# Four buffers for the split weight halves, and no page of its own for the modulation sums

## The chip, the cores and the metric

The kernel runs on one core of a Trainium2 chip. The metric is the device time in microseconds of one execution. Five engines work from queues of their own, each in the order in which the compiler put its instructions: TensorE (PE, matmuls), VectorE (DVE), ScalarE (ACT), GpSimd (POOL) and SyncE (SP), which here issues nearly all DMA transfers.

## The reference

One block of a diffusion transformer: 512 latent tokens and 256 context tokens of width 2048, all in float32.

```python
mod = silu(c) @ w_mod + b_mod                 # six chunks of 2048: shift, scale, gate (mixer), shift, scale, gate (MLP)
h = rms_norm(x, nw0) * (1 + sc_m) + sh_m      # the same for the context
p = concat(h_ctx, h_lat) @ w_in               # 2048 -> 6176
lru = conv + gated linear recurrence, both directions
gdn = conv + chunked gated delta rule, 8 heads, both directions
x = x + g_m * rms_norm(concat(lru, gdn) @ w_out, nw1)
h = rms_norm(x, nw2) * (1 + sc_f) + sh_f
x = x + g_f * rms_norm(square(relu(h @ w_ff1)) @ w_ff2, nw3)      # 2048 -> 8192 -> 2048
```

The two shift and scale rows of the mixer (chunks 0 and 1) are needed first. The other four chunks are needed later: chunk 2 scales the mixer's output, chunks 3 and 4 the MLP's input, and chunk 5 (`g_f`) only the very last sum.

## The kernel before

**Products.** Every float32 product is made of three matmuls in a rounded format (`fp32r`): each operand is split into a high and a low part, and high x high, high x low and low x high are added in one PSUM bank. For the weights the split is done on the fly. A weight piece `wr` of 128 x 1024 is loaded by SP, and each of its two halves is turned into `wh` (a cast on ACT, line 67) and `wl` (a subtraction on DVE or POOL, line 61). In the mixer's input product and in the MLP one half feeds 12 matmuls, in the output product 6. The text calls the matmuls of one half a quarter.

**The feed.** Class `Feed` (line 475) makes the halves in order for the input product, the output product and the first two MLP blocks. Before the first product it splits three halves; after the products of half c, `next` splits half c + 3 into the buffers that half c has just left, since `wh` and `wl` have three buffers each. The other MLP blocks do the same through `wpiece` (line 276), and the first modulation chunks in a loop of their own (line 328).

**Pages.** Most temporary tiles are "pages" of 128 x 512 float32, 29 buffers of one tag. A few kinds have tags of their own: five buffers `ld` for loads, four for the recurrent state, and one, `macc`, for the modulation sums.

**Modulation sums.** `modacc` (line 1144) makes one quarter f of chunks 2 to 5. It takes a tile, clears it on POOL (line 1148), loads a row of `b_mod` into it (line 1149) and adds 16 rows of weights to it with 16 DVE operations (line 64), each fed by one `ld` load of 256 KB (line 1156). For chunks 2, 3 and 4 (12 sums, made during the mixer) the running sum lies in a PSUM bank: only the first of the 16 operations reads the tile, and a copy on ACT (line 1164) brings the sum back into it at the end. For chunk 5 the sum stays in the tile. Then the tile is stored to DRAM (`accD`, line 1165). The next sum clears the same buffer, so it waits for that store.

**The gate rows.** `modrow(5, 3)` (line 1173) is called in the MLP's loop at block b == 3, right behind the call that makes the four sums of chunk 5. It loads each sum back and multiplies it with a matrix of ones (line 1181, four matmuls on PE), to spread it over all partitions. The result is used only by the last 16 sums of the kernel.

**What sets the order.** A planner in the kernel spawns the tasks of the mixer between the quarters (`slot`), and marks at each `boundary` keep an engine from running more than one to three slots ahead. The MLP from its third block on, and the sums of chunk 5, have no such marks: there the framework's scheduler places each instruction when its inputs and a buffer are there in its own model of time, and otherwise by the order of the program. Once placed, the order on an engine is fixed.

Of the kernel before, what the change touches and what calls it, by code (L numbers as in the profile page):

```python
# [8 lines left out]
F32R = mybir.dt.float32r  # L9
# [7 lines left out]
P = 128  # L17
# [14 lines left out]
def build(tc, A, out, stop=None, dump=None):  # L32
    nc = tc.nc
    V, S, G, T, SP = nc.vector, nc.scalar, nc.gpsimd, nc.tensor, nc.sync
    es = ExitStack()
    with es:
        cp = es.enter_context(tc.tile_pool(name="const", bufs=1))
        wp = es.enter_context(tc.tile_pool(name="weights", bufs=2))
        pp = es.enter_context(tc.tile_pool(name="pages", bufs=29))
        ld_n = 5  # L40

        pg = ps = es.enter_context(tc.tile_pool(name="psum", bufs=8, space=PSUM))
# [3 lines left out]
        def nm(s):  # L46
            cnt[0] += 1
            return f"{s}_{cnt[0]}"

        def page(dt=F32, tag="pg", shape=(P, 512), bufs=None):  # L50
            kw = {} if bufs is None else {"bufs": bufs}
            return pp.tile(list(shape), dt, tag=tag, name=nm(tag), **kw)

        def bank(pool=None, tag="b"):
            return (pool or ps).tile([P, 512], F32, tag=tag, name=nm("bk"))
# [7 lines left out]
        def stt(out, a, s, b, op0, op1):  # L63
            V.scalar_tensor_tensor(out=out, in0=a, scalar=s, in1=b, op0=op0, op1=op1)

        def split(src, hi, lo, lo_eng=None):
            S.copy(hi, src)  # L67
            tt(lo_eng or V, lo, src, hi.bitcast(F32), ALU.subtract)
# [43 lines left out]
        def mload(j):  # L112
            if j < len(mpieces):
                f, kind, k = mpieces[j]
                col = kind * D + f * 512
                mraw[j] = quad("mr", F32)
                SP.dma_start(mraw[j], wmod[:, k:k + 4, col:col + 512])
# [32 lines left out]
        def columns(src, n, dst):  # L150
            b = bank()
            T.transpose(b[:, :n], src[:n, :], ident[:n, :n])
            V.tensor_copy(dst[:, :n], b[:, :n])
# [122 lines left out]
        def wpiece(src, nk, cols, eng=(V, V)):  # L276
            r = wp.tile([P, 1024], F32, tag="wr", name=nm("wr"), bufs=3)
            rv = r[:, :nk * cols].rearrange("p (k f) -> p k f", f=cols)
            SP.dma_start(rv, src)
            res = []  # L280
            n = nk * cols // 2
            for i in range(2):
                h = wp.tile([P, 512], F32R, tag="wh", name=nm("wh"), bufs=3)
                l = wp.tile([P, 512], F32R, tag="wl", name=nm("wl"), bufs=3)
                split(r[:, i * n:(i + 1) * n], h[:, :n], l[:, :n], eng[i])
                hv, lv = (x[:, :n].rearrange("p (k f) -> p k f", f=cols) for x in (h, l))
                res += [(hv[:, k, :], lv[:, k, :]) for k in range(nk // 2)]
            return res
# [15 lines left out]
        def mod_cols(f, kind, pm):  # L304
            mrow, nrow = page()[:4], page()[:2]
            V.tensor_copy(mrow, pm[0][:4, :])
            S.copy(nrow, pm[1][:2, :])
            yield
            b = bank()
            bv = b[:, 0:8].rearrange("p (k j) -> p k j", j=2)  # L310
            for k in range(4):
                T.matmul(bv[:, k, :], mrow[:, k * P:(k + 1) * P], sel, start=True, stop=False)
                T.matmul(bv[:, k, :], nrow[:, k * P:(k + 1) * P], ident[:2, :2], start=False, stop=True)
            dst = (shc, scol)[kind][:, :, 4 * f:4 * f + 4]
            bm = bmod[:, kind * 16 + 4 * f:kind * 16 + 4 * f + 4]
            for j in range(2):
                tt(V, dst[:, j, :], bv[:, :, j], bm, ALU.add)
                if kind == 1:
                    stt(dst[:, j, :], dst[:, j, :], 1.0, nw0[:, 4 * f:4 * f + 4], ALU.add, ALU.mult)
            if kind == 1:  # L320
                for t in range(2):
                    yield
                    ts_ = slice(t * P, (t + 1) * P)
                    to_fm(xctx[t][f], [x[:, :, ts_] for x in Hc[f][0]], [x[:, :, ts_] for x in Hc[f][1]],
                          scol[:, 1, 4 * f:4 * f + 4], shc[:, 1, 4 * f:4 * f + 4])

        late = []
        for j, (f, kind, k0) in enumerate(mpieces):
            if k0 == 0:
                pm = [bank(pg), bank(pg)]  # L330
            r = mraw.pop(j)
            hl = []
            for i in range(3):
                h = wp.tile([P, 512], F32R, tag="wh", name=nm("wh"), bufs=3)
                l = wp.tile([P, 512], F32R, tag="wl", name=nm("wl"), bufs=3)
                split(r[:, i], h, l)
                hl.append((h, l))
            T.matmul(pm[1][:2, :], csn[:, k0 + 3, :], r[:, 3], start=k0 == 0, stop=k0 == 12)
            for i in range(3):
                k = k0 + i  # L340
                T.matmul(pm[0][:4, :], cst[:, k, :], hl[i][0], start=k == 0, stop=False)
                T.matmul(pm[0][:4, :], cst[:, k, :], hl[i][1], start=False, stop=k == 14)
            del hl, h, l
            mload(j + MB)
            if j == 2:
                while vs:
                    columns(*vs.pop(0))
            for g in list(late):
                if next(g, 0) == 0:
                    late.remove(g)  # L350
            if k0 == 12:
                late.append(mod_cols(f, kind, pm))
                next(late[-1])
        while late:
            for g in list(late):
                if next(g, 0) == 0:
                    late.remove(g)
# [35 lines left out]
        class Task:  # L393


            def __init__(self, gen, order=0, rate=None, prio=0):
                self.gen, self.order, self.rate, self.credit, self.wait, self.done = gen, order, rate, 0.0, 0, False
                self.urgent, self.prio = False, prio
# [76 lines left out]
        class Feed:  # L475
            def __init__(self, pieces):
                self.pieces, self.raws, self.parts, self.c = pieces, {}, {}, 0
                for j in range(3):
                    self.load(j)
                for c in range(3):  # L480
                    self.split(c)

            def load(self, j):
# [6 lines left out]
            def split(self, c):  # L490
                if c >= 2 * len(self.pieces):
                    return
                _, nk, cols, eng = self.pieces[c // 2]
                n = nk * cols // 2
                r = self.raws[c // 2][:, (c % 2) * n:(c % 2) * n + n]
                h = wp.tile([P, 512], F32R, tag="wh", name=nm("wh"), bufs=3)[:, :n]
                l = wp.tile([P, 512], F32R, tag="wl", name=nm("wl"), bufs=3)[:, :n]
                split(r, h, l, eng[c % 2])
                self.parts[c] = (h, l)
                if c % 2:  # L500
                    del self.raws[c // 2]
                    self.load(c // 2 + 3)
# [2 lines left out]
                return self.parts.pop(self.c)  # L505

            def next(self):
                self.split(self.c + 3)
                self.c += 1

        def run_tiles(ds):
# [632 lines left out]
        def modacc(chunk, f, after=None):  # L1144

            col = chunk * D + f * 512
            acc = seed = page(tag="macc", bufs=1)
            G.memset(acc, 0.0)
            SP.dma_start(acc[0:1, :], A["b_mod"][:, col:col + 512])
            if after is None:  # L1150
                acc = bank()
            q = []
            for k in range(17):
                if k < 16:
                    w = page(tag="ld", bufs=ld_n)
                    SP.dma_start(w, wmod[:, k, col:col + 512])
                    q.append(w)
                if k > 0:
                    stt(acc, q.pop(0), silc[:, k - 1:k], seed if k == 1 else acc, ALU.mult, ALU.add)
                    if after is not None:  # L1160
                        tc.add_manual_dep(nc.cur_bb.bb.instructions[-1], after, NOSYNC, reason="order")
                    yield 0.7, 0, 0
            if after is None:
                S.copy(seed, acc)
            SP.dma_start(accD[4 * (chunk - 2) + f], seed)
            modok.add((chunk, f))
# [90 lines left out]
        for o in orders[0] + orders[1]:  # L1257
            for k in o[1]:
                c = o[0]
# [15 lines left out]
        def big4(i):  # L1275
            if i < 3:
                xs = [pp.tile([P, 1024], F32, tag="A", name=nm("big"), bufs=A_BUFS) for _ in range(2)]
                return [xs[c // 2][:, c % 2 * 512:c % 2 * 512 + 512] for c in range(4)]
            return [page(tag="S", bufs=4) for _ in range(4)]
# [260 lines left out]
        acc = [big4(t) for t in range(4)]  # L1540
# [53 lines left out]
```

## Time and profile before

| what | value |
|---|---|
| median of 3 runs | 2808.57 us (2805.38 to 2812.1) |
| the profiled execution's own time | 2803.51 us |
| its span, first to last instruction | 2801.7 us |
| PE busy | 2654.4 us, 95% of the span |
| DVE, ACT, POOL busy | 1682.8, 1187.9, 586.1 us |
| mean granted clock of PE | 0.979 |

The page names an instruction by line, engine and operation, then output and inputs by tile name. A time in square brackets behind a row is how long the engine had been idle before it, and what ended that. The stages follow each other as: modulation chunks 0 and 1 (to about 140 us), input product and mixer (to about 1240), output product (to about 1380), MLP (to the end).

### The profile page before, as it was taken

Reading aid. Unit: us, or ns where it says so; the run is one execution under the profiler, and the core shown is the slowest. Engines: PE = TensorE matmul, PEld = TensorE weight load, DVE = VectorE, ACT = ScalarE, POOL = GpSimd, SP = SyncE. Lnnn points to the kernel's source line nnn. Section 1 sums busy time; section 2 is a strip of 40 time slices with the busy share of each in tenths; the row PEclk is TensorE's granted clock in tenths of the full one; section 3 lists DMA queues with packets and bytes.
Section 4 is the critical chain, followed back from the end, with each engine's and each line's share of the span. In section 5 each row is a group of like instructions: output and inputs, shape, how many; then the busy total and the mean of one; then the engine's idle time right before and its main releaser. Section 6 shows DMA issues by size and latency. Waiting matters only on the chain.

```text
span 2801.7 us, 39553 instructions
## 1 busy us (share of the span) xinstructions
PE 2654.4 (95%) x14253; PEld 2178.3 (78%) x14253; DVE 1682.8 (60%) x3287; ACT 1187.9 (42%) x2418; POOL 586.1 (21%) x552
## 2 busy tenths in 40 slices
PE   6989899899999998988999999999999999999998
PEld 2378797788777887776898887888888888888886
DVE  5786767777696777847598433444433444334436
ACT  4556576654556564535552222222222222222223
POOL 1155354344244354326310000000000000000002
PEclk9999999999999999989999999999999999999999
DMA  9664465566566667646778333333333333333335
GB/s 331 215 177 126 109 187 166 153 187 190 168 189 189 200 198 222 212 150 212 235 258 277 119 98 113 98 98 98 98 98 98 94 96 97 98 98 98 98 98 154
DMA packets 374968, 434.33 MB, mean 155 GB/s; under 512 B 22665, under 2 KB 212450, under 8 KB 374770
## 3 DMA queue, kind: packets, MB, share of 16 engines
q1 hardware_dynamic: 373984, 431.59, 49.6%
q8 instruction: 112, 1.84, 0.3%
q14 instruction: 86, 0.70, 0.1%
q10 hardware_dynamic: 786, 0.19, 0.0%
HBM read 401.31 MB, written 30.41 MB: 154 GB/s over the span
## 4 chain that ended last, share of the span: by engine, by line
PE 57%; DVE 4%; DMA 2%; POOL 1%; issue 1%; ACT 1%; SPq 0%; DVEq 0%; ACTq 0%; POOLq 0%
PE bk L1510 8%; PE bk L1508 8%; PE bk L1509 8%; PE bk L1497 7%; PE bk L1498 7%; PE bk L1499 7%; PE bk L1420 2%; PE bk L1419 2%; PE bk L1418 2%; PE bk L1469 1%; DVE pg L61 1%; PE bk L1468 1%; PE bk L1467 1%; DVE wl L61 1%; PE bk L524 1%
## 5 line engine op out<-in xcount | busy, mean ns | idle before, releaser
L67 ACT CAST wh<-wr 128x512 fp32r<-128x512 f32 x952 | 584.6, 618 | 1217.1 <-PE bk L1498 443.9
L61 DVE TENSOR_TENSOR wl<-wr,wh 128x512 fp32r<-128x512 f32 x642 | 464.1, 725 | 761.6 <-ACT wh L67 643.3
L61 POOL TENSOR_TENSOR wl<-wr,wh 128x512 fp32r<-128x512 f32 (+1 forms) x310 | 402.4, 1304 | 609.9 <-ACT wh L67 555.1
L1510 PE MATMUL bk<-wl,pg 128*128 128x512 f32 x960 | 373.6, 389 | 0.9 <-DVE wl L61 0.9
L1509 PE MATMUL bk<-wh,pg 128*128 128x512 f32 x960 | 373.5, 389 | 0.0
L1508 PE MATMUL bk<-wh,pg 128*128 128x512 f32 x960 | 373.5, 389 | 0.0
L1497 PE MATMUL bk<-H2h,wh 128*128 128x512 f32 x896 | 349.9, 390 | 0.0
L1499 PE MATMUL bk<-H2h,wl 128*128 128x512 f32 x896 | 349.0, 390 | 0.0
L1498 PE MATMUL bk<-H2l,wh 128*128 128x512 f32 x896 | 349.0, 390 | 0.0
L524 PE MATMUL bk<-Hlh,wh 128*128 128x512 f32 (+1 forms) x784 | 316.5, 404 | 0.0
L526 PE MATMUL bk<-Hlh,wl 128*128 128x512 f32 (+1 forms) x784 | 309.9, 395 | 1.8 <-POOL wl L61 1.8
L525 PE MATMUL bk<-Hll,wh 128*128 128x512 f32 (+1 forms) x784 | 310.1, 396 | 0.0
L61 POOL TENSOR_TENSOR big<-big,pg 128x512 f32<-128x512 f32 x9 | 12.0, 1340 | 1247.5 <-ACT pg L1570 1247.5
L1510 PEld LDWEIGHTS bk<-wl,pg 128*128 128x128 f32 x960 | 180.2, 188 | 38.8 <-DVE wl L61 1.3
L1508 PEld LDWEIGHTS bk<-wh,pg 128*128 128x128 f32 x960 | 180.2, 188 | 37.3
L1509 PEld LDWEIGHTS bk<-wh,pg 128*128 128x128 f32 x960 | 180.2, 188 | 37.2
L1498 PEld LDWEIGHTS bk<-H2l,wh 128*128 128x128 f32 x896 | 168.5, 188 | 35.4 <-issue 0.5
L1497 PEld LDWEIGHTS bk<-H2h,wh 128*128 128x128 f32 x896 | 168.6, 188 | 35.3 <-issue 0.2
L1499 PEld LDWEIGHTS bk<-H2h,wl 128*128 128x128 f32 x896 | 168.5, 188 | 35.2
L526 PEld LDWEIGHTS bk<-Hlh,wl 128*128 128x128 f32 (+1 forms) x784 | 148.4, 189 | 35.8 <-POOL wl L61 2.3
L524 PEld LDWEIGHTS bk<-Hlh,wh 128*128 128x128 f32 (+1 forms) x784 | 149.1, 190 | 30.9 <-ACT pg L1071 0.2
L525 PEld LDWEIGHTS bk<-Hll,wh 128*128 128x128 f32 (+1 forms) x784 | 148.8, 190 | 29.9
(346 smaller groups left out, 4514.5 us busy)
## 6 DMA issues: line engine op xcount, KB each, us to landing
wr<-in_w_ff SPq DMA_DIRECT2D x272, 512.0 KB
wr<-in_w_in SPq DMA_DIRECT2D x144, 512.0 KB
ld<-in_w_mod SPq DMA_DIRECT2D x256, 256.0 KB
mr<-in_w_mod SPq DMA_DIRECT2D x32, 1024.0 KB
wr<-in_w_out SPq DMA_DIRECT2D x64, 512.0 KB
pg<-vkD SPq DMA_DIRECT2D x88, 128.0 KB
ld<-in_x SPq DMA_DIRECT2D x32, 256.0 KB
vkD<-pg SPq DMA_DIRECT2D x24, 256.0 KB
```

Source lines behind the costliest of these rows:

```text
L61: e.tensor_tensor(out=out, in0=a, in1=b, op=op)
L67: S.copy(hi, src)
L524: T.matmul(pt[:m, :n], wh, a, start=k == 0, stop=False)
L525: T.matmul(pt[:m, :n], wh, b, start=False, stop=False)
L526: T.matmul(pt[:m, :n], wl, a, start=False, stop=k == 15)
L1418: T.matmul(bk[t], mh[:, s_], h, start=st, stop=False)
L1497: T.matmul(bk[c], w[kk][0][:, s_], hh, start=k == 0, stop=False)
L1498: T.matmul(bk[c], w[kk][0][:, s_], hl_, start=False, stop=False)
L1499: T.matmul(bk[c], w[kk][1][:, s_], hh, start=False, stop=k == 15)
L1508: T.matmul(o, ah, h, start=k == 0, stop=False)
L1509: T.matmul(o, al, h, start=False, stop=False)
L1510: T.matmul(o, ah, l, start=False, stop=k == 3)
```

## The change

Three things are changed.

1. `wh` and `wl` have four buffers each in place of three. The feed splits four halves before the first product, and half c + 4 after the products of half c.
2. The tag `macc` is gone. The modulation sums take an ordinary page. For chunks 2 to 4 that page is let go after the first of the 16 operations, and the copy at the end takes another page.
3. The ordinary pages are 28 in place of 29, which makes up, with the `macc` page, for the two added buffers.

```diff
-        pp = es.enter_context(tc.tile_pool(name="pages", bufs=29))
+        pp = es.enter_context(tc.tile_pool(name="pages", bufs=28))
...
-                h = wp.tile([P, 512], F32R, tag="wh", name=nm("wh"), bufs=3)
-                l = wp.tile([P, 512], F32R, tag="wl", name=nm("wl"), bufs=3)
+                h = wp.tile([P, 512], F32R, tag="wh", name=nm("wh"), bufs=4)
+                l = wp.tile([P, 512], F32R, tag="wl", name=nm("wl"), bufs=4)
...
-                for c in range(3):
+                for c in range(4):
                     self.split(c)
...
             def next(self):
-                self.split(self.c + 3)
+                self.split(self.c + 4)
                 self.c += 1
...
         def modacc(chunk, f, after=None):
 
             col = chunk * D + f * 512
-            acc = seed = page(tag="macc", bufs=1)
+            acc = seed = page()
             G.memset(acc, 0.0)
             SP.dma_start(acc[0:1, :], A["b_mod"][:, col:col + 512])
             if after is None:
                 acc = bank()
...
                 if k > 0:
                     stt(acc, q.pop(0), silc[:, k - 1:k], seed if k == 1 else acc, ALU.mult, ALU.add)
+                    if after is None:
+                        seed = None
                     if after is not None:
                         tc.add_manual_dep(nc.cur_bb.bb.instructions[-1], after, NOSYNC, reason="order")
                     yield 0.7, 0, 0
             if after is None:
+                seed = page()
                 S.copy(seed, acc)
             SP.dma_start(accD[4 * (chunk - 2) + f], seed)
```

Instructions move with it, mostly by one split: on each engine the split of a half stands one quarter earlier among the other work. At three places more than that moves.

**The sums of chunk 5 on DVE.** Before, the 64 operations of line 64 (`macc<-ld,silc,macc`) stand scattered from the first MLP blocks on. Here are the first of them, beside the halves `wl` of the second MLP block:

```order
L61 TENSOR_TENSOR wl_15281<-wr_15146,wh_15280 128x512
L61 TENSOR_TENSOR pg_15259<-pg_15257,pg_15258 128x256
L64 SCALAR_TENSOR_TENSOR macc_17336<-ld_17339,silc,macc_17336 128x512
L61 TENSOR_TENSOR wl_15299<-wr_15190,wh_15298 128x512
L64 SCALAR_TENSOR_TENSOR macc_17336<-ld_17341,silc,macc_17336 128x512
L61 TENSOR_TENSOR wl_15315<-wr_15190,wh_15314 128x512
```

The last of the 64 then stands beside the 609th half, 55 halves ahead of the one whose products PE does just before the gate rows (the 664th; halves are counted from the kernel's first). With the change the first of the sums stands behind the 656th half, in the products of the MLP's third block with `w_ff2`:

```order
L61 TENSOR_TENSOR big_15822<-big_15822,bk_17046 128x512
L61 TENSOR_TENSOR S_15824<-S_15824,bk_17047 128x512
L61 TENSOR_TENSOR wl_17165<-wr_17158,wh_17164 128x512
L64 SCALAR_TENSOR_TENSOR pg_17348<-ld_17351,silc,pg_17348 128x512
L64 SCALAR_TENSOR_TENSOR pg_17348<-ld_17353,silc,pg_17348 128x512
L64 SCALAR_TENSOR_TENSOR pg_17348<-ld_17356,silc,pg_17348 128x512
L61 TENSOR_TENSOR wl_17203<-wr_17200,wh_17202 128x512
```

From there 27 of them stand among 12 halves and 12 sums of the MLP's output (`big`, `S`). The other 37 stand in one run behind `wl_17633`, the 668th half, whose beginning is:

```order
L64 SCALAR_TENSOR_TENSOR pg_17400<-ld_17429,silc,pg_17400 128x512
L61 TENSOR_TENSOR wl_17629<-wr_17626,wh_17628 128x512
L64 SCALAR_TENSOR_TENSOR pg_17400<-ld_17432,silc,pg_17400 128x512
L61 TENSOR_TENSOR wl_17633<-wr_17626,wh_17632 128x512
L64 SCALAR_TENSOR_TENSOR pg_17400<-ld_17435,silc,pg_17400 128x512
L64 SCALAR_TENSOR_TENSOR pg_17400<-ld_17438,silc,pg_17400 128x512
L64 SCALAR_TENSOR_TENSOR pg_17400<-ld_17441,silc,pg_17400 128x512
```

and whose end is:

```order
L64 SCALAR_TENSOR_TENSOR pg_17504<-ld_17548,silc,pg_17504 128x512
L64 SCALAR_TENSOR_TENSOR pg_17504<-ld_17551,silc,pg_17504 128x512
L61 TENSOR_TENSOR pg_17562<-bk_17560,ld_17558 128x512
L61 TENSOR_TENSOR pg_17570<-bk_17568,ld_17566 128x512
L61 TENSOR_TENSOR pg_17578<-bk_17576,ld_17574 128x512
L61 TENSOR_TENSOR pg_17586<-bk_17584,ld_17582 128x512
L61 TENSOR_TENSOR wl_17663<-wr_17660,wh_17662 128x512
```

The four rows `pg<-bk,ld` take the results of the gate rows, so the last sum now stands just ahead of the gate rows' use. SP's queue moved with it: 59 of the 64 `ld` loads stand among the weight pieces of the same stretch, and the last 32 of them between two neighbouring weight pieces.

**The gate rows on PE.** Their place did not move. With the change (line 1184 is the old 1181, lines 1500 to 1502 the old 1497 to 1499, 1512 and 1513 the old 1509 and 1510):

```order
L1512 MATMUL bk_17275<-wh_17316,pg_16431 128x512
L1513 MATMUL bk_17275<-wl_17317,pg_16430 128x512
L1184 MATMUL bk_17560<-ld_17556,ones 128x512
L1184 MATMUL bk_17568<-ld_17564,ones 128x512
L1184 MATMUL bk_17576<-ld_17572,ones 128x512
L1184 MATMUL bk_17584<-ld_17580,ones 128x512
L1500 MATMUL bk_17588<-H2h_13512,wh_17594 128x512
```

`wh_17316` is the 664th half, `wh_17594` the 665th: the gate rows stand between the third block's second product and the next block's first.

**A modulation sum of the mixer on DVE.** The first operation of the sixth of the 12 sums (chunk 3), at about 713 us in the trace, stands before the change like this (`negL` and `ss` are rows of the delta rule and of a norm):

```order
L61 TENSOR_TENSOR pg_7683<-pg_7683,bk_7716 128x512
L64 SCALAR_TENSOR_TENSOR bk_7816<-ld_7817,silc,macc_7813 128x512
L64 SCALAR_TENSOR_TENSOR pg_7763<-bk_7764,negL,pg_7668 128x128 x4
L745 TENSOR_SCALAR ss_7751<-ss_7751 128x8
L64 SCALAR_TENSOR_TENSOR bk_7816<-ld_7819,silc,bk_7816 128x512
```

and with the change like this:

```order
L61 TENSOR_TENSOR pg_7693<-pg_7693,bk_7724 128x512
L64 SCALAR_TENSOR_TENSOR pg_7773<-bk_7774,negL,pg_7678 128x128 x4
L745 TENSOR_SCALAR ss_7761<-ss_7761 128x8
L185 TENSOR_SCALAR rqy_7806<-ss_7761 128x8
L64 SCALAR_TENSOR_TENSOR rqt_7807<-rqy_7806 128x8
```

The first operation (`bk_7825<-ld_7826,silc,pg_7822`) now stands 16 other operations later, behind the whole norm. The second and the third of the 12 sums moved in the same way by 16 and 12 operations, the fifth by 11, the seventh 13 earlier; the other seven by one at most.

More of the change, by code (lines that the diff above doesn't have):

```diff
@@ L333, in build @@
             for i in range(3):
-                h = wp.tile([P, 512], F32R, tag="wh", name=nm("wh"), bufs=3)
-                l = wp.tile([P, 512], F32R, tag="wl", name=nm("wl"), bufs=3)
+                h = wp.tile([P, 512], F32R, tag="wh", name=nm("wh"), bufs=4)
+                l = wp.tile([P, 512], F32R, tag="wl", name=nm("wl"), bufs=4)
                 split(r[:, i], h, l)
@@ L495, in split @@
                 r = self.raws[c // 2][:, (c % 2) * n:(c % 2) * n + n]
-                h = wp.tile([P, 512], F32R, tag="wh", name=nm("wh"), bufs=3)[:, :n]
-                l = wp.tile([P, 512], F32R, tag="wl", name=nm("wl"), bufs=3)[:, :n]
+                h = wp.tile([P, 512], F32R, tag="wh", name=nm("wh"), bufs=4)[:, :n]
+                l = wp.tile([P, 512], F32R, tag="wl", name=nm("wl"), bufs=4)[:, :n]
                 split(r, h, l, eng[c % 2])
```

## The prediction

> **What bounds the kernel now.** I read the page first, then who PE waited for, then PE's own rows in order of time.
>
> ```profile
> span 2801.7 us, 39553 instructions
> PE 2654.4 (95%) x14253; PEld 2178.3 (78%) x14253; DVE 1682.8 (60%) x3287; ACT 1187.9 (42%) x2418; POOL 586.1 (21%) x552
> ...
> PE bk L255 <- DVE pg L64: 19.8, 7, 5.7
> PE bk L951 <- DVE pg L927: 11.8, 4, 9.2
> PE bk L526 <- POOL wl L61: 8.8, 9, 1.8
> PE bk L524 <- ACT wh L67: 4.2, 6, 1.3
> PE bk L1420 <- POOL wl L61: 3.5, 4, 1.3
> PE bk L342 <- DVE wl L61: 3.4, 7, 0.8
> PE bk L1469 <- DVE wl L61: 3.4, 5, 1.4
> PE bk L526 <- DVE wl L61: 3.2, 4, 1.2
> PE bk L1181 <- DMA ld<-accD: 2.6, 1, 2.6
> PE bk L1510 <- DVE wl L61: 0.9, 1, 0.9
> ```
>
> PE sets the end: it is idle for 147 us (2801.7 - 2654.4) and works the rest. Each row of the waits gives the total, the number and the longest. The seven rows on `wh` and `wl` are what a fourth buffer can touch, and they sum to 27.4 us, 1% of the span. The other waits are for chains of DVE (transposes, the delta rule). So the buffers alone are worth little, and anything else that the change moves by tens of us decides.
>
> The rows of PE show where it stands, and windows show its pace and clock (columns: window, PE busy and count, PEld, DVE, ACT, POOL, granted clock, DMA share, GB/s):
>
> ```profile
> 480.45 0.36 PE L578 MATMUL bk<-pg,pg 128*128 128x256 f32 x1 [2.66 <-DVE pg L61]
> ...
> 720.21 0.77 PE L578 MATMUL bk<-pg,pg 128*128 128x512 f32 x1 [2.13 <-DVE pg L64]
> ...
> 1080.99 0.31 PE L951 MATMUL bk<-pg,A 32*32 32x32 f32 x4 [9.23 <-DVE pg L927]
> ...
> 1693.99 2.74 PE L1181 MATMUL bk<-ld,ones 128*128 128x512 f32 x6
> 1699.31 1.54 PE L1181 MATMUL bk<-ld,ones 128*128 128x512 f32 x2 [2.58 <-DMA ld<-accD]
> ...
> 1701.08 0.63 PE L1498 MATMUL bk<-H2l,wh 128*128 128x512 f32 x1
> ...
> 1238.00:1246.00 8.00, 7.55 (x21) 5.58 (x20) 1.69 (x3) 1.85 (x4) 2.74 (x3) 0.51 0.01 3
> 1699.00:1704.00 5.00, 4.69 (x12) 3.23 (x13) 1.05 (x2) 0.00 (x0) 0.00 (x0) 0.66 0.79 252
> 2000.00:2400.00 400.00, 400.00 (x1766) 331.23 (x1765) 172.76 (x267) 113.40 (x187) 0.00 (x0) 1.00 0.32 98
> ```
>
> In the long MLP stretch PE never waits and does a matmul in 400 / 1766 = 0.2265 us, so a quarter of 12 takes 2.72 us. A buffer more gains nothing there. After a wait the clock is about half for a while: between 1699 and 1704 us the mean is 0.66, so of 5 us 0.34 x 5 = 1.7 us are lost; 8 us at 0.51 (1238 to 1246) lose 3.9.
>
> **Part 1: the fourth buffer.** It adds no instruction; it lets a split run one quarter earlier. That quarter is 2.72 us in the MLP's full rows, half of that where the rows have 256 columns or a half feeds 6 matmuls. Every wait in the seven rows is at most 1.8 us long, near or under this, so nearly all single ones should go. I leave out the 3.4 us of L342: that stage has DMA as its bound, by the second of these rows.
>
> ```profile
> DMA  9664465566566667646778333333333333333335
> GB/s 331 215 177 126 109 187 166 153 187 190 168 189 189 200 198 222 212 150 212 235 258 277 119 98 113 98 98 98 98 98 98 94 96 97 98 98 98 98 98 154
> ```
>
> Of the other 24.0 us I keep 3 for places in the context rows where several waits follow each other, since there the split is short of throughput and one buffer is used up once: 21. The clock falls after a wait, too: for the three longest of them (1.8, 1.4, 1.4) I add an estimated 1.7 us each, from the row at 1699: 5. Together -26, with 0 and -29 (24.0 + 5) as its ends.
>
> **Part 2: the modulation sums of the mixer.** Before, the next sum had to wait until the last was stored.
>
> ```profile
>   DMA accD<-macc: 94.7, 10
> ...
>   DMA macc<-in_b_mod: 16.0, 5
> ...
> 472.26 1.76 DVE L64 SCALAR_TENSOR_TENSOR bk<-ld,silc,macc 128x512 f32<-128x512 f32 x1 [4.61 <-DMA macc<-in_b_mod]
> ...
> 718.36 0.76 DVE L64 SCALAR_TENSOR_TENSOR bk<-ld,silc,macc 128x512 f32<-128x512 f32 x1 [4.93 <-DMA macc<-in_b_mod]
> ```
>
> The first two rows say what POOL and DVE waited for at this tile: POOL stood 94.7 us before the clearing, with `wl` halves queued behind it, and DVE 16.0 us for the row of biases. Two of PE's waits follow directly: 480.45 and 720.21, after DVE's 4.61 and 4.93 us. The page ends the wait for the store, and in the order two of these first operations stand 16 others later, so DVE should not meet them early any more. That is 2.66 + 2.13, and 1.7 of clock at each: -8. The L951 group behind the 9.23 us wait stands 13 to 16 matmuls later now, about 3.5 us: -3.5.
>
> What it costs: a page must be free twice per sum, where one had lain ready. The trace has no page wait. From above I bound it by DVE's 16.0 us at the old tile, from below by 0, and take 0, since few other rows moved in the mixer.
>
> Parts 1 and 2 are -38 at most of their likely values. Some is given back: what PE does not lose on a weight it may lose at the next DVE chain, and DVE is packed before 1081 us. I take half, -19, with ends at -38 and -4.
>
> **Part 3: the sums of chunk 5.** This term decides.
>
> ```profile
> L64 DVE SCALAR_TENSOR_TENSOR macc<-ld,silc,macc x64: 741/750/754, 1434.1 to 1541.5; 128x512 f32<-128x512 f32 x64
> ...
> 1499.66 2.32 DVE L64 SCALAR_TENSOR_TENSOR macc<-ld,silc,macc 128x512 f32<-128x512 f32 x3
> 1501.89 0.68 DVE L61 TENSOR_TENSOR wl<-wr,wh 128x512 fp32r<-128x512 f32 x1
> 1502.50 2.32 DVE L64 SCALAR_TENSOR_TENSOR macc<-ld,silc,macc 128x512 f32<-128x512 f32 x3
> ...
> 1541.50 0.75 DVE L64 SCALAR_TENSOR_TENSOR macc<-ld,silc,macc 128x512 f32<-128x512 f32 x1 [1.22 <-DMA ld<-in_w_mod]
> ...
> 1670.74 1.88 DVE L61 TENSOR_TENSOR big<-big,bk 128x512 f32<-128x512 f32 x3
> 1672.54 0.68 DVE L61 TENSOR_TENSOR S<-S,bk 128x512 f32<-128x512 f32 x1
> 1673.14 0.68 DVE L61 TENSOR_TENSOR wl<-wr,wh 128x512 fp32r<-128x512 f32 x1
> ...
> 1517.78 0.33 SPq L1165 DMA_DIRECT2D accD<-macc  x1
> 1521.04 0.53 POOL L1148 MEMSET macc<- 128x512 f32 x1 [25.06 <-DVE S L1514]
> ...
> 1537.24 0.46 SPq L1156 DMA_DIRECT2D ld<-in_w_mod  x1
> ...
> 1695.77 0.34 SPq L1170 DMA_DIRECT2D ld<-accD  x1
> ```
>
> Before, the 64 operations ended at 1542 us, 150 us ahead of the gate rows at 1694. In the new order they begin behind the 656th half. With four buffers its cast waits for the products of the 652nd, 12 quarters before the gate rows: 1694.0 - 12 x 2.72 = 1661.4. Four sums of the output (2.40 us, 1670.74 to 1673.14), the cast and the subtraction later, 1664.8, the first one starts. Per operation DVE needs (1501.89 - 1499.66) / 3 = 0.74 us, per half 0.61 (1501.89 to 1502.50), per sum of the output 0.60. So up to the run of 37: 27 x 0.74 + 12 x 0.61 + 12 x 0.60 = 34.5, to 1699.3. PE came to the gate rows at 1694.0 and stands.
>
> The run: DVE alone needs 37 x 0.74 = 27.4. But each operation needs a load into one of five buffers. From issue (1537.24) to use (1541.50) one took 4.3 us, and the load of a sum 3.5 (1695.77 to 1699.31). With the operation and the issue, 0.74 + 0.2, five loads go round in 4.4 to 5.2 us: 0.9 to 1.05 each. I take 0.95 for the 32 that are not there yet: 32 x 0.95 + 5 x 0.74 = 34, to 1733.4. Ends: 27.4, and 49 at the pace of the old stretch, 43 us for 32 operations by this window of the tile:
>
> ```profile
> 1499.50:1542.50 43.00, 23.99 (x32) 0.00 (x0) 0.53 (x1) 1.00 0.82 274
> ```
>
> The Trainium skill (DMA: Bandwidth & Descriptors, Specifications) gives about 358 GB/s of HBM bandwidth per core; by that a load of 256 KB takes 0.73 us, DVE would set the pace, the run would take 27.4 us and the forecast would be 6.6 us lower. The highest slice here shows 331 GB/s, 0.79 us a load, but round trips with five buffers bind first.
>
> After the run come store and reload: 3.3 us (1517.78 to 1521.04) and 3.5. The last gate row then runs at 1740.2 and PE goes on at 1741, where it went on at 1701.1: +40. The clock stays low somewhat longer than after the old 2.58 us wait, between 0 and 2.2 us (3.9 - 1.7): +1. The Trainium skill (TensorE: Matmul & The Clock Gate, Part 1) has full clock back after one busy window of about 3.4 us, which would make it 0; the 8 us at 0.51 differ from that. Nothing covers these 41 us, because PE's next product stands behind the gate rows. Ends: +33 and +56.
>
> **Sum.** +41 - 19 = +22. The profiled execution took 2803.5 us (2801.7 of span and 1.8 around it): 2825.5. The three timed runs have a median 5.1 us higher, so for the median 2830.
>
> **The rivals.** (a) PE never stands at the gate rows, because the 64 operations come early enough, and only the gains stay: 2808.6 - 19 = 2790, faster. It needs them done within the 32.6 us of the 12 quarters; DVE alone would need 64 x 0.74 = 47. Against it stand all rows above; for it only that waits could let DVE run ahead. 5%. (b) Gains whole, run at DVE's pace: -38 + 33 (+2 for stragglers) leaves 2806, no change. For it speaks that PE's weight waits are spread and mostly local. 9%. (c) Pages bind in the mixer: 12 sums with a page wait at each end, 24 waits of 0.7 us or more on DVE's or ACT's queue, 16 us: 2846. Against: ACT's and POOL's other rows kept their order. 12%. (d) The buffers and the page do nothing, since DVE's chains take all back: 2808.6 + 41 - 4 = 2846. 13%. My forecast: 61%.
>
> **Numbers.** 0.2% (5.6 us) is about what a measurement tells from no change here. Faster: (a), and 1% of the forecast's low tail, 6%. No change: (b), 9%. Slower: 85%. The forecast's own range is 2815 to 2846 (part 3 from +33, gains from -30; part 3 +52, gains -14); with (b), (c) and (d) 2807 to 2853 holds 8 in 10.
>
> **What would show it.** Right: at L1184 (the old L1181) one wait of about 40 us for a load of `accD`, behind an unbroken run of L64 on DVE with PE idle; waits for `wh` and `wl` down from 27.4 to some 6 us; no wait of DVE or POOL for a store of the old sum. Wrong: the gate rows without a wait over 10 us, or operations of chunk 5 before 1600 us; new waits for pages at the clearing or the copy; weight waits as before.

## The result: 1.6% slower

The changed kernel takes 2850.43 us (median of 4 runs, 2849.47 to 2851.32), the kernel before 2806.98 us in the same comparison: a ratio of 1.0161, 95% interval [1.0141, 1.0182], about +43 us. Foretold were 2830 us (+22) and a range of 2807 to 2853. The direction and the one large term were right; the gain that was to pay for half of it did not come. The measured time lies 3 us inside this range and outside the forecast's own, 2815 to 2846.

The page of the changed kernel gives its span, PE's work and PE's granted clock in 40 slices:

```profile
span 2849.6 us, 39560 instructions
PE 2665.5 (94%) x14253; PEld 2192.1 (77%) x14253; DVE 1690.8 (59%) x3287; ACT 1185.5 (42%) x2418; POOL 582.2 (20%) x552
PEclk8999899999999999989999997999999999999999
```

The span grew by 47.9 us. PE does the same 14253 matmuls in 11.1 us more of busy time (2665.5 against 2654.4) and is idle for 184.1 us in place of 147.3. The slice with a 7 in the clock is the place of the new wait.

What PE waited for in the changed kernel (total, number, longest), the rows of the gate rows, of DVE's chains and of the weight halves. The output product's lines 1418 to 1420 are 1421 to 1423 now, and 1467 to 1469 are 1470 to 1472:

```profile
PE bk L1184 <- DMA ld<-accD: 40.5, 3, 39.0
PE bk L255 <- DVE pg L64: 24.9, 7, 8.2
PE bk L1038 <- DVE pg L64: 9.3, 3, 4.8
PE bk L1423 <- DVE wl L61: 4.9, 3, 3.3
PE bk L526 <- DVE wl L61: 4.3, 3, 2.5
PE bk L342 <- DVE wl L61: 4.2, 9, 0.8
PE bk L524 <- ACT wh L67: 0.8, 1, 0.8
PE bk L1423 <- POOL wl L61: 0.7, 1, 0.7
PE bk L1472 <- DVE wl L61: 0.6, 2, 0.4
PE bk L526 <- POOL wl L61: 0.2, 1, 0.2
```

The seven rows on `wh` and `wl` sum to 15.7 us where the seven rows quoted of before summed to 27.4. So the fourth buffer did take waits for weights away. That is less than forecast, where some 6 us were to be left. The longest of those left are longer (3.3 and 2.5 us, before 1.8), and the transposes of line 255 wait 5 us more for DVE in the row shown.

**At the gate rows.** PE's rows of the changed kernel around them:

```profile
1702.43 0.39 PE L1513 MATMUL bk<-wl,pg 128*128 128x512 f32 x1
1741.86 2.08 PE L1184 MATMUL bk<-ld,ones 128*128 128x512 f32 x2 [39.03 <-DMA ld<-accD]
1745.13 3.98 PE L1184 MATMUL bk<-ld,ones 128*128 128x512 f32 x4 [1.19 <-DMA ld<-accD]
1749.33 1.22 PE L1184 MATMUL bk<-ld,ones 128*128 128x512 f32 x2 [0.23 <-DMA ld<-accD]
1749.98 0.79 PE L1500 MATMUL bk<-H2h,wh 128*128 128x512 f32 x1
1750.62 0.40 PE L1501 MATMUL bk<-H2l,wh 128*128 128x512 f32 x1
```

and what DVE did meanwhile (the 64 operations of chunk 5, then the beginning and the end of the unbroken run):

```profile
L64 DVE SCALAR_TENSOR_TENSOR pg<-ld,silc,pg x64: 744/752/754, 1671.6 to 1740.9; 128x512 f32<-128x512 f32 x64
...
1707.51 3.91 DVE L64 SCALAR_TENSOR_TENSOR pg<-ld,silc,pg 128x512 f32<-128x512 f32 x5
1712.58 2.33 DVE L64 SCALAR_TENSOR_TENSOR pg<-ld,silc,pg 128x512 f32<-128x512 f32 x3 [1.15 <-DMA ld<-in_w_mod]
...
1737.76 3.90 DVE L64 SCALAR_TENSOR_TENSOR pg<-ld,silc,pg 128x512 f32<-128x512 f32 x5 [0.37 <-DMA ld<-in_w_mod]
```

PE came to the gate rows at 1702.8 and did the second matmul behind them (line 1501, before 1498) at 1750.62, 47.8 us later; before it came at 1693.99 and did the same matmul at 1701.08, 7.1 us later. The difference is 40.7 us. The run lasted from 1707.5 to 1741.7, 34.1 us for 37 operations.

What the first gate row waited for is its reload, not its sum. SP's rows of the four stores and reloads, the first and the last of each:

```profile
1690.38 0.33 SPq L1168 DMA_DIRECT2D accD<-pg  x1
...
1738.54 0.33 SPq L1173 DMA_DIRECT2D ld<-accD  x1
...
1741.69 0.33 SPq L1168 DMA_DIRECT2D accD<-pg  x1
...
1746.44 0.32 SPq L1173 DMA_DIRECT2D ld<-accD  x1
```

The first sum was stored at 1690.38, before PE came. Its reload was issued only at 1738.54, because it stands behind the loads of chunk 5 on SP's queue. The last gate row then waited for the last sum, stored at 1741.69.

**Ahead of the gate rows.** PE reached them 8.8 us later than before (1702.8 against 1694.0) where 19 us earlier was forecast. Windows of PE show what that is made of (window, busy and count, granted clock, DMA share, GB/s), first before, then the changed kernel:

```profile
0.00:300.00 300.00, 251.46 (x1453) 0.95 0.65 207
300.00:600.00 300.00, 274.85 (x1875) 0.96 0.53 155
600.00:1400.00 800.00, 744.36 (x4573) 0.97 0.64 198
...
0.00:1693.99 1693.99, 1560.62 (x9445) 0.97 0.61 190
```

```profile
0.00:300.00 300.00, 255.01 (x1452) 0.91 0.65 207
300.00:600.00 300.00, 269.29 (x1817) 0.93 0.52 150
600.00:1400.00 800.00, 744.72 (x4528) 0.97 0.64 196
...
0.00:1702.80 1702.80, 1570.23 (x9445) 0.96 0.59 182
```

The last row of each counts the same 9445 matmuls, up to the gate rows: PE was idle for 1693.99 - 1560.62 = 133.4 us before and 1702.80 - 1570.23 = 132.6 us after. Idle time is the same within 1 us, although 12 us of waits for weights went: they came back as other waits. Up to the gate rows the sum of PE's waits by what ended them is, without those for `wh` and `wl`, 3.8 us larger for DVE, 5.6 for DMA and 3.0 for ACT and POOL together. And the same matmuls took 9.6 us more of busy time. The clock was lower in two stages: 0.91 for 0.95 up to 300 us, 0.93 for 0.96 from 300 to 600. By the counts the first of them cost next to nothing, since PE had done 1452 matmuls at 300 us and 1453 before; from 300 to 600 us it did 58 fewer, from 600 to 1400 us 45 fewer.

One row stands out in the second of these stages. DVE and POOL of the changed kernel, beside PE's next wait:

```profile
413.43 1.30 POOL L61 TENSOR_TENSOR wl<-wr,wh 128x512 fp32r<-128x512 f32 x1 [5.11 <-DMA ld<-in_w_mod]
...
417.44 0.54 POOL L1148 MEMSET pg<- 128x512 f32 x1
417.93 5.05 POOL L61 TENSOR_TENSOR wl<-wr,wh 128x512 fp32r<-128x512 f32 x4
422.93 1.28 POOL L61 TENSOR_TENSOR pg<-ld,pg 128x512 fp32r<-128x512 f32 x1
...
419.41 7.25 DVE L64 SCALAR_TENSOR_TENSOR bk<-ld,silc,pg 128x512 f32<-128x512 f32 x1 [4.83 <-DMA pg<-in_b_mod]
...
427.57 2.08 PE L1038 MATMUL bk<-pg,A 128*128 128x128 f32 x8 [4.84 <-DVE pg L64]
```

An operation that has a median of 0.76 us in this kernel and 1.9 us at most in the kernels without this event took 7.25 us, beside an unbroken stretch of POOL in which four `wl` halves stand in a row; PE then waited 4.84 us. Comparing when PE reached the same matmul, the changed kernel was 3.5 us behind before the event (416 us) and 10.7 us behind after it (444 us). The distance does not stay so: it is 14.1 us at 555 us and 4.6 us at 1088 us, and 8.8 us at the gate rows.

### The profile page after: what moved, and what is told of

The parts are those of the page before. It is cut to its first block, busy times and chain, and to the rows that moved or that the text cites. A ratio compares the mean times of both kernels' runs of the same rounds, so it can differ in the third digit from the quotient of the medians.

```text
span 2849.6 us, 39560 instructions
## 1 busy us (share of the span) xinstructions
PE 2665.5 (94%) x14253; PEld 2192.1 (77%) x14253; DVE 1690.8 (59%) x3287; ACT 1185.5 (42%) x2418; POOL 582.2 (20%) x552
## 4 chain that ended last, share of the span: by engine, by line
PE 50%; DVE 2%; DMA 1%; issue 0%; POOL 0%; ACT 0%; DVEq 0%; SPq 0%; ACTq 0%; POOLq 0%
PE bk L1511 8%; PE bk L1512 8%; PE bk L1513 8%; PE bk L1501 7%; PE bk L1500 7%; PE bk L1502 7%; DMA ld<-in_w_mod 1%; PE bk L1472 1%; PE bk L1470 1%; PE bk L1471 1%; DVE pg L64 1%; PE bk L1423 1%; PE bk L1422 1%; PE bk L1421 1%; DVE wl L61 0%
## 5 line engine op out<-in xcount | busy, mean ns | idle before, releaser
L61 POOL TENSOR_TENSOR big<-big,pg 128x512 f32<-128x512 f32 x9 | 11.5, 1296 | 1206.3 <-ACT pg L1573 1206.3
```

What stands on the lines that cost most here:

```text
L61: e.tensor_tensor(out=out, in0=a, in1=b, op=op)
```

## The experiments

Each was compared with the kernel before on the same chip. Theory G is about the gate rows, the theories M, B, P and C (the clock) about the rest.

**Chunk 5 on a tag of its own.** The changed kernel with one line more, and a page less:

```diff
-        pp = es.enter_context(tc.tile_pool(name="pages", bufs=28))
+        pp = es.enter_context(tc.tile_pool(name="pages", bufs=27))
...
-            acc = seed = page()
+            acc = seed = page() if after is None else page(tag="macc", bufs=1)
```

> The changed kernel, but the four sums of chunk 5 get a tag of their own with one buffer again (the mixer's sums stay on ordinary pages; 27 ordinary pages make up for it). In the order the 64 operations stand beside halves 558 to 609 again, as before the change. Theory G (the 39 us wait at the gate rows comes from these operations standing behind half 655): the wait falls from 39 us to under 5 us and the time from 2850 to about 2811. Theory M (the rest of the loss, 8.8 us up to the gate rows, comes with the fourth buffer or with the mixer's pages): 2811 to 2816 remain, above the 2807 of before. Prediction as it stood (mixer gains 19): 2790. Rival to G (the gate rows wait for something else, the reload itself): the wait stays over 30 us and the time near 2850.

Measured: 2808.88 us, ratio 1.0017 [1.0003, 1.0030]. Its gate rows:

```profile
1698.40 2.74 PE L1184 MATMUL bk<-ld,ones 128*128 128x512 f32 x6
1704.25 1.24 PE L1184 MATMUL bk<-ld,ones 128*128 128x512 f32 x2 [3.11 <-DMA ld<-accD]
```

The wait fell from 39.0 to 3.1 us and the ratio by 1.44% of 2807, 40 us. Theory G stands: the whole of the large loss comes from where the sums of chunk 5 stand, and that comes from the page they take. What is left shows no gain. PE comes to the gate rows 4.4 us later than before (1698.40), although the operation of 7.25 us is in this kernel too.

**The gate rows two blocks later.**

```diff
             if b == 3:
                 for _ in mods((5,), last):
                     pass
-                gf = modrow(5, 3)
+            if b == 5:
+                gf = modrow(5, 3)
```

> The changed kernel, but the gate rows are called in the MLP's block 5 in place of block 3; the four sums stay in block 3. In the order the gate rows now stand behind half 727 and the sums spread over halves 655 to 677. Theory G: PE no longer stands for the sums; the 40 us go, except what DVE now holds back of the halves among which the sums stand: there DVE has 64 x 0.74 + 22 x 0.61 + 22 x 0.60 = 74 us of work in 22 x 2.72 = 60 us of PE, so 0 to 20 us of waits for wl: 2811 to 2831. Rival (the sums cost PE the same wherever they stand, since DVE and the loads set the pace): waits for wl of 35 to 40 us, 2845 to 2850.

Measured: 2819.67 us, ratio 1.0052 [1.0033, 1.0071], between the ends of theory G. What PE waited for from 1690 to 1900 us:

```profile
PE bk L1500 <- ACT wh L67: 9.8, 2, 8.6
PE bk L1184 <- DMA ld<-accD: 2.7, 1, 2.7
```

The 39 us became 9.8 us of waits for halves; 64 operations and their loads stand among 22 halves there. So the price depends on how much other work of PE lies between the sums and their use; it isn't a fixed price of the sums.

**Four buffers alone.** Before, with the bufs and the lookahead of the change; the old page for the sums kept, 27 ordinary pages.

```diff
-        pp = es.enter_context(tc.tile_pool(name="pages", bufs=29))
+        pp = es.enter_context(tc.tile_pool(name="pages", bufs=27))
...
-                h = wp.tile([P, 512], F32R, tag="wh", name=nm("wh"), bufs=3)
+                h = wp.tile([P, 512], F32R, tag="wh", name=nm("wh"), bufs=4)
...
-                self.split(self.c + 3)
+                self.split(self.c + 4)
```

> Before, with the four buffers alone: the page of the modulation sums is kept, 27 ordinary pages make up for the two added buffers. The sums of chunk 5 stand where they stood before. Theory M-buffers (the 8.8 us lost up to the gate rows come with the fourth buffer, by a PE clock that falls more often): about 2816, with waits for wh and wl down from 27 to about 15 us and more half-clock time than before. Theory M-pages (they come with the pages in the mixer): the buffers alone are at 2807 or below. Prediction as it stood: 21 to 26 us faster, 2781 to 2786, less half given back: 2794.

Measured: 2813.11 us, ratio 1.0032 [1.0021, 1.0043]. The fourth buffer, which was to gain 21 us or more, loses 9. Windows of this kernel's PE:

```profile
0.00:300.00 300.00, 255.60 (x1437) 0.91 0.66 206
300.00:600.00 300.00, 274.45 (x1870) 0.94 0.54 152
600.00:1400.00 800.00, 737.64 (x4461) 0.96 0.64 194
```

The clock is low in the same two stages, and a little in the third, without the change's pages and without its chunk 5. By the counts most is lost in the third stage (4461 matmuls, before 4573). At the gate rows this kernel is 13 us late:

```profile
1706.97 2.73 PE L1181 MATMUL bk<-ld,ones 128*128 128x512 f32 x6
```

Up to there PE was busy for 1572.8 us and idle for 134.1 us, before for 1560.6 and 133.4. So here too the loss is busy time and not idle time, and no operation of 7.25 us is in this kernel: the longest first operation of a sum takes 1.72 us.

**The pages alone.** The changed kernel with three buffers and a lookahead of three (28 pages).

> The changed kernel with three buffers in place of four: the sums on ordinary pages, 28 of these. The sums of chunk 5 stand behind half 654, as in the changed kernel one half earlier. Theory G: a wait at the gate rows of about 39 us. Theory M-pages: also 9 us lost up to the gate rows, 2855. Theory M-buffers: nothing lost up to there, 2846 or less. Prediction as it stood for the pages: 11 us gained in the mixer, half given back, 2841.

Measured: 2842.32 us, ratio 1.0133 [1.0108, 1.0158]: the wait at the gate rows is there (39.0 us), and nothing else is lost: PE comes to the gate rows at 1694.97, 1 us later than before. Its clock up to 300 us is 0.92, low as in the changed kernel, so the low clock of the first stage is not what the fourth buffer loses. Against the changed kernel's 1.0161 this is 0.28% less, some 8 us, for the fourth buffer with the same number of pages (the two intervals overlap a little). The first operation of its modulation sums took its usual time:

```profile
414.33 0.76 DVE L64 SCALAR_TENSOR_TENSOR bk<-ld,silc,pg 128x512 f32<-128x512 f32 x1 [1.66 <-issue]
```

**Two pages fewer, nothing else.** Before with 27 ordinary pages in place of 29.

> Before, with 27 ordinary pages in place of 29 and nothing else. The four buffers alone (with these 27 pages) were 0.32% slower than before, and this separates pages from buffers. Theory B (the fourth buffer costs the 9 us, since PE's many short waits for weights become fewer and longer waits for DVE, and its clock is halved after a long one): no change here, within 0.1% of before, half-clock time as before (some 106 us up to the gate rows). Theory P (two pages fewer hold DVE and ACT up): 6 to 9 us slower than before, like the four buffers.

Measured: 2804.67 us, ratio 1.0006 [0.9994, 1.0017]. Pages cost nothing here. So the 9 us of the four buffers are the buffers' own, less at most 0.17%.

**Four buffers, still three ahead.** As four buffers alone, with the lookahead of before.

> Before, with four buffers and 27 pages, but the feed still splits only three halves ahead. Theory B-early (what costs is that splits stand one quarter earlier in front of the chains that PE waits for): the loss of 9 us goes where the feed works, some 3 us of the modulation stage may stay: 0 to 3 us above before. Theory B-buffer (the buffers themselves cost it, wherever the splits stand) or P (the pages): 6 to 9 us above before.

Measured: 2810.18 us, ratio 1.0027 [1.0015, 1.0039]. Theory B-early predicted that most of the loss would go; it did not. With the old page kept, the loss is there at either depth. But the edit does not keep the order of three ahead: with DVE's operations put in order of their start and compared by tile name, 285 of the 3287 stand elsewhere than before, and only 110 elsewhere than with four buffers and four ahead. So this run does not part the depth from the buffers. (Its profiled execution took 2819 us, 9 more than its median, so its times aren't used.)

**The mixer's pages alone.** The changed kernel without its other two effects: three buffers, 29 ordinary pages, chunk 5 on its own tag.

> The changed kernel's mixer sums on ordinary pages, and neither of the other two effects: three buffers, 29 ordinary pages, and chunk 5 on a tag of its own with one buffer. Theory: the mixer's pages alone gain something, 2 to 5 us (four buffers with them 2809, without them 2813): 2800 to 2803 where before has 2804.4. Prediction as it stood: 11.5 us, half of it given back, 2799. Rival (the difference was within the noise, and waits for pages eat the gain): 2804 or more.

Measured: 2804.03 us, ratio 1.0002 [0.9991, 1.0014]. The rival was right: nothing gained. DVE's waits for the row of biases fell from 16.0 us to this row

```profile
DVE bk L64 <- DMA pg<-in_b_mod: 3.7, 2, 2.7
```

and POOL's waits for the store are gone from the mixer, and the time is the same. So other work set the end there; which work it was is not shown.

**Two depths.** The kernel with chunk 5 on its own tag (1.0017), whose feed looks four ahead only in the context rows and in front of the MLP:

```diff
-                for c in range(4):
+                for c in range(3):
                     self.split(c)
+                self.s = 3
...
-                self.split(self.c + 4)
                 self.c += 1
+                ahead = 4 if self.c < 72 or self.c >= 422 else 3
+                while self.s < self.c + ahead:
+                    self.split(self.s)
+                    self.s += 1
```

> The changed kernel with chunk 5 on a tag of its own (27 pages), whose feed looks four halves ahead only where that shortened the time in the traces (the context rows and the last pieces in front of the MLP) and three halves ahead otherwise. Theory B-early: the losses of 8 us (from 321 to 443 us) and of some 7 us (from 1090 to 1300 us) do not arise, the gains of 4 to 7 us at the two places stay: 2795 to 2802. Rival (the places of gain and loss are chance of one profile, or the buffers cost it anyhow): 2805 to 2812.

Measured: 2793.38 us, ratio 0.9961 [0.9947, 0.9974]: faster than both kernels, and 0.56% (16 us) below the same kernel with four ahead everywhere. The first operation of its first modulation sum, and POOL beside it:

```profile
415.96 1.68 DVE L64 SCALAR_TENSOR_TENSOR bk<-ld,silc,pg 128x512 f32<-128x512 f32 x1 [4.83 <-DMA pg<-in_b_mod]
...
414.49 5.54 POOL L61 TENSOR_TENSOR wl<-wr,wh 128x512 fp32r<-128x512 f32 x4
```

Here the operation takes 1.68 us, where the three kernels with four ahead everywhere and the mixer's sums on pages have 7.25, and POOL has the same four halves in a row beside it. Between the traces of the two kernels (spans 2806.1 and 2792.5 us) PE is 7.4 us ahead right behind this place; the other 6 come in pieces of 1 to 3 us that no single row explains.

**Work in PE's waits.** If a long wait costs twice, once as idle time and once as a slower clock behind it, then matmuls of constants in the wait should save the second part. They are put ahead of eight transposes, in the bank that these overwrite; the output is not touched:

```diff
+        fill = {37: 18, 41: 14, 43: 32, 60: 15, 63: 15, 64: 8, 69: 8, 82: 42}
+        ncall = []
+
         def transp(src):
             b = bank()
+            for _ in range(fill.get(len(ncall), 0)):
+                T.matmul(b[:, :P], ones, ident, start=True, stop=True)
+            ncall.append(0)
```

> Before, with small matmuls of constants put on PE ahead of eight transposes that wait 1.7 to 7.3 us for DVE (at 467, 501, 535, 750, 828, 843, 921 and 1238 us): 8 to 42 of 128x128, 0.15 us each, 1 to 6.5 us per place, a little less than the wait. They write the bank that the transposes overwrite; nothing else changes. Theory C (a window of 3.41 us in which PE works less than half is followed by one at half clock, so that a long wait costs twice): the half-clock windows behind these waits go (13 windows of 3.41 us from 440 to 1260 us before, some 8 fewer), half of their length is gained, and what a filler outlasts its wait is lost: 8 to 14 us faster, 2789 to 2795. Rival (the clock follows something else, the kind of matmul or the power of the stretch, or the waits are the whole cost): the windows stay, no gain or a loss of up to 5 us.

Measured: 2803.68 us, ratio 0.9999 [0.9987, 1.0011]. The last filler and the stretch behind it:

```profile
1229.38 9.54 PE L258 MATMUL bk<-ident,ones 128*128 128x128 f32 x84
...
1239.00:1247.00 8.00, 7.08 (x34) 1.00 0.12 37
```

The clock behind it is 1.00, where it was 0.51 before from 1238 to 1246, and the half clock is gone as well behind the other five of the eight places that had it. But no time was gained. A matmul of the filler took 9.54 / 42 = 0.23 us, not 0.15, so the fillers outlasted their waits, this one 7.28 us by 2.2, all eight by 5.6 us. In this kernel half-clock windows stand at 568, 670 and 1107 us, where the kernel before has none, and the wait at 1081 us grew from 9.23 to 10.36 us. That work in the wait keeps the clock up behind it is shown; that it pays is not.

**The same work with four buffers.** The fillers in the kernel with four buffers alone:

> The same matmuls of constants in the kernel with four buffers alone (27 pages, the old page for the sums), which took 2813 without them; its waits at the eight places are 1.6 to 2.4 us longer at three of them. Theory C together with theory B (the fourth buffer's loss is the clock behind longer waits): a gain of 12 to 18 us, larger than the same fillers bring before, to 2795 to 2801, so that most of the 9 us between the two is gone. If the loss has another cause: the same gain as before's, and the 9 us stay.

Measured: 2806.17 us, ratio 1.0008 [0.9996, 1.0020], against 1.0032 [1.0021, 1.0043] without the fillers. The same fillers that bring nothing before bring 0.24% (7 us) here, about half of what was expected, and the difference to before is no longer measurable. They change little besides: 17 of DVE's 3287 operations stand elsewhere than without them. Its windows:

```profile
0.00:300.00 300.00, 254.99 (x1445) 0.93 0.66 207
300.00:600.00 300.00, 283.78 (x2004) 0.97 0.54 155
600.00:1400.00 800.00, 754.41 (x4732) 0.98 0.65 198
```

0.97 and 0.98 where it was 0.94 and 0.96 (busy time and counts hold the fillers here). So a large part of what the fourth buffer loses goes with the half clock behind long waits.

**The same work with two depths.** The fillers in the kernel with two depths:

> The same matmuls of constants in the kernel that looks four halves ahead in two places and three elsewhere (2793.4 without them). Theory C: 8 to 14 us faster, 2779 to 2785, the fastest version. Rival: no gain, 2791 to 2798.

Measured: 2791.20 us, ratio 0.9955 [0.9942, 0.9969], against 0.9961 without: no difference.

**Fillers that fit.** The same with 12, 14, 26, 11, 10, 8, 8 and 30 matmuls, and 19 more ahead of the wait at 1074 us.

> The kernel with two depths of lookahead again, with the matmuls of constants sized by what one took (0.23 us, not 0.15): 8 to 30 of them at the eight transposes, and 19 ahead of the 5.4 us wait at 1074 us. In the runs before this the fillers removed the half-clock windows behind all eight places, but outlasted their waits by some 5 us in all (9.5 us of filler for a wait of 7.3 us, 4.2 for 3.7). Theory C (the clock windows are a real cost, and the missing gain was the overrun): 3 us of overrun less and 5 us of half clock less behind 1074 us: 2783 to 2788 where 2791 and 2793 were. Rival (what is gained on the clock is lost again because PE then waits the longer for the same chains of DVE): 2789 to 2794.

Measured: 2790.28 us, ratio 0.9950 [0.9935, 0.9964]. The rival was nearer: its interval holds the two before it. This is the fastest version, some 13 us below before, nearly all of it from the two depths.

## Why the prediction was right and where it was wrong

**Part 3, the sums of chunk 5: right, +41 forecast, +40.7 measured in the traces, 40 by the experiment that undoes it alone.** The steps hold one by one. The first operation was to come 12 quarters ahead of the gate rows and a few operations later, 1664.8 against 1694.0, 29.2 us ahead; it came at 1671.6 against 1702.8, 31.2 ahead. Up to the run: 34.5 forecast, 35.9 measured (1671.6 to 1707.5). The run itself at 0.95 us for each load: 34 forecast, 34.1 measured, and the loads set its pace, by the waits for `ld<-in_w_mod` between its pieces and this window of DVE's operations:

```profile
1705.00:1735.00 30.00, 23.45 (x32) 0.50 0.90 302
```

The Trainium skill (DMA: Bandwidth & Descriptors, Specifications) has about 358 GB/s, by which DVE alone would have set the pace and the run taken 27.4 us; the window moves 302 GB/s. Whether the round trip of five buffers or the DMA engines, 0.90 busy, hold it there was not separated. From the end of the run to PE's next product 7.6 us were forecast, 8.3 measured. What the prediction did not have is that all four reloads stand behind the loads: PE stood already at the first gate row, whose sum had long been stored.

**Part 1, the fourth buffer: this step failed.** "Nearly all single ones should go", 21 us of waits and 5 of clock, was the term. Measured on its own it is a loss of 7 to 9 us (0.32% with the old page, less the 0.06% measured for two pages fewer; 0.28% with the new ones). The waits went as far as 27.4 to 15.7 us, so half of the mechanism was there. Two things were wrong behind it. First, half of the gain was allowed to be given back to DVE's chains; it was all given back (idle time 133.4 and 132.6 us), and only a third of that to DVE. Second, the clock was counted as a gain of 1.7 us for three waits that go, and never as a cost of the waits that grow. Many short waits leave the clock up, a few long ones don't. The fillers bear this out: they give back 0.24% of the 0.32% in the kernel with four buffers, and nothing in the one before. In the changed kernel itself PE falls back by 7.2 us across one event, the operation of 7.25 us and the wait behind it, which no row of before could have shown. That this event makes the 8.8 us lost ahead of the gate rows is not shown: four buffers alone lose 13 us there without it, and chunk 5 on its own tag loses 4.4 us with it.

**Part 2, the mixer's sums: mis-sized.** 11.5 us were summed, half of them kept; alone the pages give 0.02% [-0.09, 0.14], under 3 us. The two stalls of line 578 at 480 and 720 us did go, as forecast, and the wait of 9.23 us at 1081 became 4.59 in the changed kernel and 6.6 with the pages alone. It bought nothing measurable. A reading and an expectation were wrong. Of the 94.7 us that POOL stood for the store, 65.5 us are two waits at the sums of chunk 5 in the MLP, and only 29.2 lie in the mixer. And DVE's wait for the row of biases, 16.0 us before, which was to go, is still 14.8 us in the changed kernel. With four buffers the pages seem to gain 4 us (2813.11 to 2808.88; the intervals overlap). What was taken as 0, the wait for pages, was too small to measure.

**The rivals.** (c) and (d) were both put at 2846, nearest in time. (c), waits for pages, is out: 27 pages cost nothing. (d), that DVE's chains take all back (13%), was nearest in mechanism, though it had no loss beside it. (a) is out with the wait of 39 us, (b) with the run of 34.1 us and the gains that did not come. That the range holds the result is owed to (c) and (d), which widened it to 2853. The lower end of the forecast's own range is also misadded: 2808.6 + 33 - 30 is 2812 and not 2815. The sum is then 40 for part 3, 7 to 9 for part 1 and 0 for part 2, 47 to 49 where the medians say 43; the profile says 47.9.

**What stays open.** Why three ahead with four buffers helps in one setting (the two depths, with the sums on pages) and not in the other (the old page kept) is not settled. Nor is it settled why the four-buffer kernels are 3 to 7 us behind already at 140 us, where DMA is the bound, and why most of that is made up by 300 us.

## What to carry to other kernels

Before giving up a tile of its own for a shared pool, look where the order puts what uses it: taking a page moved 64 operations to some 100 halves later, and cost 40 us although no engine had more to do for it. A short wait mostly costs itself alone; one that empties more than half a clock window costs up to 1.7 us of slower work besides. So a buffer more, which takes some waits and lengthens others, is to be counted with its clock, and its lookahead tried per stage rather than everywhere. Waits on a list are not time: 12 us of them went, and the idle time stayed.

## What was not expected of the hardware

**The clock follows windows of 3.41 us.** In the traces of all these kernels the granted clock changes only on a grid of 3.41 us and only between full and half, from its first record at about 20 us on. Worked out from PE's rows and the clock's records of thirteen kernels (all but four buffers with three ahead): of the windows whose preceding one had PE busy for under 40%, 282 of 282 were at half clock; at 40 to 50% it is 69% of 75, at 50 to 60% 26% of 106, at 60 to 90% 12% of 589, at 90% and more 1% of 9562. So a wait of a little over 2 us that falls into one window was always enough, and one of 1.7 to 2 us mostly. The Trainium skill (TensorE: Matmul & The Clock Gate, Part 1) gives the window and the two clocks as the traces have them; but it puts the fall behind one idle window, and here a window idle for six tenths sufficed. Fillers at 0.23 us a matmul took the half clock away behind their waits, but cut to fit these waits they still gave no gain that could be measured.

**A DVE operation held for 7.25 us beside POOL.** The operation at 419.41 us reads two tiles of SBUF, as all of line 64's first operations of a sum do, and took 7.25 us, 10 times its usual time, while POOL had operations back to back from 413.4 to 427.9 us. It is at the same place in all three kernels with four ahead everywhere and the mixer's sums on pages (7.25 us in each), and not in the others (1.9 us at most). The Trainium skill (SBUF — State Buffer, Who interferes with whom) has a rule for it: a DVE instruction with two SBUF inputs contends with a GpSimd one that reads SBUF, and their shared port pair is an exclusive lock. That fits, but it is not enough: in the kernel with two depths POOL's stretch is the same, its four halves in a row took 5.54 us in place of 5.05, and the operation took 1.68 us. That it is this port, and what makes the difference, was not tested by a run.
